# Large products as Strassen blocks of seven half products, in four passes over the tokens, with transposes finished by DMA

## The chip, the core and the metric

The kernel runs on one core of one Trainium2 chip. A core has TensorE (PE, matmuls into PSUM; PEld is its weight load), VectorE (DVE), ScalarE (ACT), GpSimd (POOL) and SyncE (SP, which here issues all DMAs), and 16 DMA engines that move data between HBM and SBUF. The engines run side by side, each through its own list of instructions in a fixed order, and wait for one another by semaphores. The metric is the device time of one execution in microseconds, as the median of several runs.

## The reference, cut to what matters

One layer of a decoder trunk over 4096 tokens of 1024 features. A projection gives u, v (768 columns each), queries q_x (256) and a gate (1024). A gated spatial mixing and a 4-head cross-attention into a memory of 256 tokens stand side by side, both are multiplied by the SiLU of the gate and sent through an output projection, residual and layer norm.

```python
proj = jnp.einsum('bsd,de->bse', x, a_w_in[j])
u, v, q_x, gate = split_cols(proj, [TOK_WIDTH, TOK_WIDTH, XATTN_WIDTH, MIX_WIDTH])
tok = chunked_spatial_gating(u, v, a_w_s[j], a_b_s[j])
...
xo = memory_cross_attention(q_x, mem_k, mem_v)
mixed = jnp.concatenate([tok.astype(x.dtype), xo.astype(x.dtype)], axis=-1) * jax.nn.silu(gate)
y = jnp.einsum('bse,ed->bsd', mixed, w_out[i]).astype(x.dtype)
x = layer_norm(ALPHA * x + y, ln_g[i], ln_b[i])
```

The spatial gating takes GELU of u and v, normalises v in groups of 128 features, multiplies it with a causal 128 x 128 matrix within each chunk of 128 tokens, and multiplies the result with u.

## The kernel before

[...] To keep precision, every operand is split into a high part (a cast on ScalarE, L48) and a low part (a subtraction on VectorE, L49), and each product is made of three matmuls: high x high, high x low, low x high (`mm3`, L93 to L101). The contraction over 1024 features is 8 steps of 128.

Work goes over 16 blocks of 256 tokens, in three phases:

1. Phase 1 (p1) computes v and u by tokens (`by_token`: 2 halves of 128 tokens, 2 x 384 columns, tile `pair`), then GELU, the group norm (`v_norm`), the mixing (`mix`, L194) and the product with u. The result is transposed to features on partitions by VectorE in 32 x 32 blocks, 16 instructions for each half of a block (`block_transpose`, L119, tile `zt`), and stored to HBM (`z1_d`).
2. Phase 2 (p2) computes the gate by features (`by_feature`, 256 tokens as columns, tile `single`), and the attention: queries (`q_part`), scores (`scores`, L315), softmax, the transpose of the probabilities (L119, tile `pt`), their split into `pT` (L48, L49) and the product with the values (`attend`, L337). Attention of one block is spread between the gate products of the same and the next block.
3. Phase 3 (p3) does the output projection by tokens (512 columns), residual and layer norm.

Weights stay in SBUF (`wt`), and their columns are replaced by the next phase's while the former phase still runs. x is loaded from HBM in phases 1 and 2 and split again each time. A scheduler that simulates the program sets the order of the instructions on each engine; on the chip each engine follows that order and only waits. SP is one such list: a DMA that waits for its data holds back all DMAs behind it.

## Time and profile before

| | us |
|---|---|
| median of 3 runs | 1515.41 |
| lowest and highest run | 1514.56, 1518.41 |
| span of the profiled execution (first to last instruction) | 1513.3 |
| TensorE busy | 1462.3 (97%) |
| VectorE busy | 1082.4 (72%) |
| ScalarE busy | 446.8 (30%) |
| GpSimd busy | 207.2 (14%) |
| DMA, mean rate | 98 GB/s |

Busy time counts an engine's own instructions; matmuls are pipelined, so a busy TensorE is not one at its peak. The granted clock is given as a share of 2.4 GHz. A stretch of the profile is named by microseconds from the span's start. Phase 1 ends near 600 us and phase 2 near 1145 us in this execution.

### The profile page before, as it was taken

What the parts mean: (1) busy time and instruction counts of PE and PEld (TensorE: products, weight loads), DVE (VectorE), ACT (ScalarE), POOL (GpSimd) and SP (SyncE); (2) the same over time, 40 slices, a digit from 0 to 9 for tenths busy, and PEclk for the clock granted to TensorE, in tenths of its full rate; (3) what the DMA queues carried; (4) which work ended last, traced back from release to release, by engine and by line L of the source; (5) the groups of instructions that cost most, each with busy time, mean ns of one, the idle gap of its engine ahead of it and who ended that gap; (6) DMA issues with size and microseconds to landing.
All of it is one profiled execution on the core that took longest, in us unless ns stands there. A gap on an engine that the chain in (4) does not pass through costs nothing.

```text
span 1513.3 us, 24060 instructions
## 1 busy us (share of the span) xinstructions
PE 1462.3 (97%) x9392; PEld 1386.7 (92%) x9392; DVE 1082.4 (72%) x2606; ACT 446.8 (30%) x850; POOL 207.2 (14%) x149
## 2 busy tenths in 40 slices
PE   8999999999999999989999999999998999999997
PEld 8999999999999999889999999999997888888886
DVE  7767777777767777877888877777775656566564
ACT  5222222211232223454544444554441011011010
POOL 1000000000000000222222222222220100000000
PEclk9999999999999999999999999999999999999999
DMA  7222222211222224332233323222234544444331
GB/s 253 63 57 57 65 68 57 64 52 49 63 68 70 66 64 129 93 95 93 75 100 110 95 94 99 86 92 83 86 105 154 174 139 135 143 144 141 133 132 56
DMA packets 96466, 147.71 MB, mean 98 GB/s; under 512 B 8160, under 2 KB 40416, under 8 KB 96352
## 3 DMA queue, kind: packets, MB, share of 16 engines
q1 hardware_dynamic: 96352, 146.18, 30.7%
q8 instruction: 73, 1.20, 0.3%
q14 instruction: 41, 0.34, 0.1%
HBM read 100.01 MB, written 46.14 MB: 97 GB/s over the span
## 4 chain that ended last, share of the span: by engine, by line
PE 64%; DVE 24%; ACT 5%; issue 3%; DMA 2%; POOL 2%; SPq 0%; DVEq 0%; POOLq 0%; ACTq 0%
PE pair L99 55%; DVE pt L119 14%; PE single L99 5%; DVE zt L119 2%; POOL p L326 2%; PE single L194 2%; PE pair L315 2%; ACT p L323 2%; DVE xt L49 1%; DVE pT L49 1%; ACT xt L48 1%; DVE zx L344 1%; ACT L323 1%; DMA raw<-xT 1%; DVE wt L49 1%
## 5 line engine op out<-in xcount | busy, mean ns | idle before, releaser
L99 PE MATMUL pair<-wt,xt 128*128 128x384 f32 (+1 forms) x4560 | 886.4, 356 | 6.4 <-ACT wt L48 6.4
L99 PEld LDWEIGHTS pair<-wt,xt 128*128 128x128 f32 x4560 | 813.9, 189 | 74.4 <-ACT wt L48 6.4
L99 PE MATMUL single<-xt,wt 128*128 128x256 f32 x3888 | 473.6, 281 | 2.0 <-DVE xt L49 1.8
L99 PEld LDWEIGHTS single<-xt,wt 128*128 128x128 f32 x3888 | 463.9, 189 | 4.4 <-DVE xt L49 4.0
L119 DVE STREAM_TRANSPOSE pt<-p 32x256 f32<-32x256 f32 x512 | 223.2, 436 | 12.8 <-POOL p L326 5.7
L48 ACT CAST xt<-raw 128x512 fp32r<-128x512 f32 x196 | 112.7, 621 | 362.3 <-PE pair L99 204.0
L119 DVE STREAM_TRANSPOSE zt<-u 32x192 f32<-32x192 f32 x512 | 189.2, 370 | 6.9
L49 DVE TENSOR_TENSOR xt<-raw,xt 128x512 fp32r<-128x512 f32 x196 | 131.2, 691 | 32.2 <-ACT xt L48 31.3
L412 DVE SCALAR_TENSOR_TENSOR rr<-xr,pair 128x512 f32<-128x512 f32 x62 | 39.9, 683 | 130.2 <-PE pair L99 119.4
L182 POOL TENSOR_TENSOR rs<-rs,mhalf 128x6 f32<-128x6 f32 x32 | 43.8, 1370 | 530.9 <-DVE rs L181 500.2
L307 POOL TENSOR_TENSOR z<-z,g 128x512 f32<-128x512 f32 x48 | 73.3, 1527 | 273.4 <-ACT g L300 237.2
L199 DVE SCALAR_TENSOR_TENSOR u<-single,bs,u 128x256 f32<-128x256 f32 x96 | 40.5, 478 | 79.2 <-ACT u L258 77.6
L48 ACT CAST pT<-pt 128x1024 fp32r<-128x1024 f32 x32 | 33.5, 1047 | 160.5 <-DVE pt L119 160.5
L326 POOL TENSOR_TENSOR p<-p,sm 128x1024 f32<-128x1024 f32 x32 | 60.0, 1894 | 150.5 <-DVE sm L325 131.6
L417 POOL TENSOR_TENSOR rs<-rs,mhalf 128x1 f32<-128x1 f32 x32 | 29.0, 905 | 341.2 <-DVE rs L416 308.5
L184 DVE TENSOR_SCALAR vg<-vg,mv,rs 128x128 f32<-128x128 f32 x192 | 52.2, 342 | 32.2 <-POOL rs L182 32.0
L315 PE MATMUL pair<-kst,qs 128*128 128x256 f32 x256 | 43.2, 291 | 26.7 <-DVE qs L163 25.8
L173 ACT ACTIVATE vg<-pair 128x768 f32<-128x768 f32 x32 | 26.0, 814 | 134.4 <-DVE st L177 89.4
L315 PEld LDWEIGHTS pair<-kst,qs 128*128 128x128 f32 x256 | 35.3, 192 | 30.3 <-DVE qs L163 29.2
L323 ACT ACTIVATE p<-pair,nm 128x256 f32<-128x256 f32 x128 | 58.6, 484 | 0.2
L48 ACT CAST vn<-vg 128x768 fp32r<-128x768 f32 x32 | 26.7, 836 | 98.8 <-DVE vg L184 74.8
L258 ACT ACTIVATE u<-pair 128x768 f32<-128x768 f32 x32 | 25.9, 810 | 91.9 <-PE pair L99 91.9
(56 smaller groups left out, 814.2 us busy)
## 6 DMA issues: line engine op xcount, KB each, us to landing
raw<-xT SPq DMA_DIRECT2D x128, 256.0 KB, 3.4
raw<-zd SPq DMA_DIRECT2D x64, 256.0 KB, 3.5
xr<-x SPq DMA_DIRECT2D x32, 512.0 KB, 3.5
out<-rr SPq DMA_DIRECT2D x62, 256.0 KB, 2.6
z1d<-zt SPq DMA_DIRECT2D x32, 384.0 KB, 2.9
z<-z1d SPq DMA_DIRECT2D x48, 256.0 KB, 2.9
zd<-z SPq DMA_DIRECT2D x48, 256.0 KB, 2.4
raw<-w_in SPq DMA_DIRECT2D x20, 256.0 KB, 3.3
```

Source lines behind the costliest of these rows:

```text
L48: nc.scalar.copy(hi, src)
L49: eng.tensor_tensor(lo, src, r(hi), op=ALU.subtract)
L99: nc.tensor.matmul(o, stat(sh, k), mv(mh, k), start=(k == 0 and sh == 0 and mh == 0), stop=(k == KD - 1 and sh == 1))
L119: nc.vector.transpose(dst[j:j + 32, :, i:i + 32], src[i:i + 32, :, j:j + 32])
L182: nc.gpsimd.tensor_tensor(rs, rs, mhalf, op=ALU.pow)
L184: nc.vector.tensor_scalar(vg[:, g, :], vg[:, g, :], mv[:, g, 0:1], rs[:, g:g + 1], op0=ALU.subtract, op1=ALU.mult)
L199: nc.vector.scalar_tensor_tensor(u[:, :, gs], ps[:, j], bs[:, g:g + 1], u[:, :, gs], op0=ALU.add, op1=ALU.mult)
L307: nc.gpsimd.tensor_tensor(z, z, g, op=ALU.mult)
L315: nc.tensor.matmul(pv[:, h, :], qs[:, h, c * P:(c + 1) * P], kst[:, i, h, :], start=(i == 0), stop=(i == 1))
L323: nc.scalar.activation(p[:, h, :], pv[:, h, :], AF.Exp, bias=nm[:, h:h + 1], scale=SCALE, accum_out=sm[:, h:h + 1])
L326: nc.gpsimd.tensor_tensor(p, p, sm.unsqueeze(2).broadcast_to([P, HEADS, M]), op=ALU.mult)
L412: nc.vector.scalar_tensor_tensor(rr[:, cs], xr[:, cs], ALPHA, y, op0=ALU.mult, op1=ALU.add)
```

## The change

The four large products (u, v, queries and gate from x; output from the mixed features) are computed by a Strassen scheme (the Winograd form with 7 products and 15 additions). For a block of 256 tokens the left operand is cut into 2 x 2 quarters (128 tokens x 512 features), the weights into quarters of 512 features x n columns. Seven parts of each are formed (`x_parts`, `w_parts`: 4 additions each on GpSimd), split into high and low, and 7 products over 512 features (`product`, 12 matmuls each) go to three PSUM accumulators, whose sums are finished on ScalarE, VectorE and GpSimd (`gemm`).

All seven weight parts of a product fill SBUF (`arena`, 8 slots of 16 KB a partition), so the work is cut into four passes over all tokens, `places` saying where each pass's weights lie:

1. g = 0: the first 384 columns of v and of u, and the queries. It also forms the weight parts of passes 2 and 3 on the side (`prepare_slice`) and stores them in HBM (`w_d`).
2. g = 1: the other 384 columns of v and u, and the gate of the attention. It stores the seven parts of x in HBM (`x_d`, 3.67 MB a block) and prepares the weight parts of pass 4.
3. the gate of the 768 mixed features (384 columns a half) and the attention. The parts of x come back from HBM (`load_x`), unsplit work is not repeated.
4. the output projection, residual and norm.

Transposes are made in two steps: VectorE transposes 32 x 32 blocks in place of all 128 partitions in one instruction (`transposed`), and DMA moves the blocks to their places in HBM (`scatter`, four DMAs with pieces of 256 bytes; the queries of pass 1 with pieces of 128 bytes in eight), from where they are loaded again: the queries (`q_d`), the probabilities (`p_d`), the attention gate (`gx_d`) and the gated features (`z_d`).

```diff
-    def mm3(outs, stat, movs, ks=range(KD)):
...
+    def product(acc, t, w, first):
+        for k in range(KH):
+            for i, (a, b) in enumerate(((0, 0), (0, 1), (1, 0))):
+                nc.tensor.matmul(acc, t[:, a, k, :], w[:, b, k, :], start=first and k == 0 and i == 0,
+                                 stop=k == KH - 1 and i == 2, skip_group_check=True)
...
+        ax = acc("accx")
+        product(ax, xs[0], ws[0], True)
+        s1 = cs()
+        nc.scalar.copy(s1, ax)
+        aw = acc("accw")
+        product(aw, xs[1], ws[1], True)
+        u2 = cs()
+        nc.vector.tensor_tensor(u2, aw, s1, op=ALU.add)
...
+        product(aw, xs[4], ws[4], False)
+        nc.vector.tensor_tensor(s5, aw, s5, op=ALU.add)
+        done(1, 1, s5)
...
+    def x_parts(r0, r1):
+        a11, a21 = r0[:, :, :P], r0[:, :, P:]
+        a12, a22 = r1[:, :, :P], r1[:, :, P:]
+        s1, s2, s3, s4 = (sum_tile() for _ in range(4))
+        tt = nc.gpsimd.tensor_tensor
+        yield a11
+        tt(s1, a21, a22, op=ALU.add)
+        tt(s2, s1, a11, op=ALU.subtract)
+        yield s2
...
+    def parts_of(src, make):
...
+        for part in make(*load_pair(src[:, :KH, :], src[:, KH:, :])):
+            t = ring()
+            split(t[:, 0], t[:, 1], part)
+            tiles.append(t)
...
+    def first_weights():
+        for j in range(WIDTH[0] // P):
+            js = slice(j * P, (j + 1) * P)
+            for i, part in enumerate(w_parts(*load_pair(wl[SLICE0[0] + j, 0], wl[SLICE0[0] + j, 1]))):
+                w = view(places[0][i], WIDTH[0])
+                split(w[:, 0, :, js], w[:, 1, :, js], part)
...
+    def prepare_slice(n):
...
+            t = ring()
+            split(t[:, 0], t[:, 1], part)
+            nc.sync.dma_start(w_d[g][i][:, :, :, js], f(t))
...
+    def scatter(dst, src):
...
+        dv = dst.rearrange("k (j i) (q s) -> q i (k j) s", j=4, q=4)
+        for q in range(4):
+            nc.sync.dma_start(dv[q], src[q * 32:(q + 1) * 32].rearrange("i j c t -> i j (c t)"))
...
-    def block_transpose(dst, src):
-        """dst[c, g, t] = src[t, g, c] for every g, as 32 x 32 blocks."""
-        for i in range(0, P, 32):
-            for j in range(0, P, 32):
-                nc.vector.transpose(dst[j:j + 32, :, i:i + 32], src[i:i + 32, :, j:j + 32])
...
+                    nc.vector.tensor_reduce(nm, ps, axis=AX.X, op=ALU.max)
+                    nc.vector.tensor_scalar(nm, nm, -SCALE, None, op0=ALU.mult)
+                    p = sum_tile().rearrange("p k c -> p (k c)").rearrange("p (h m) -> p h m", h=2)
...
+                    nc.gpsimd.tensor_tensor(p, p, sm.unsqueeze(2).broadcast_to([P, 2, M]), op=ALU.mult)
+                    transposed(pts[hp], p.rearrange("p h m -> p (h m)"), c)
+            for hp in range(2):
+                scatter(p_d[b % 2][4 * hp:4 * hp + 4], pts[hp])
+
+        def weights_of(b):
+            nc.sync.dma_start(f(pT[:, 1]), p_d[b % 2].rearrange("k p t -> p k t"))
+            split(pT[:, 0], pT[:, 1], f(pT[:, 1]))
...
+            gemm(psum, xs, ws, 384, done)
+            scatter(z_d[b][:NH], zt)
+            attend(b, gx)
+            if b + 1 < NB:
+                scores(b + 1)
+                weights_of(b + 1)
```

The pool `ringp` holds 9 part tiles (two more than a block's seven), `raw` 3 tiles, `sums` 3 tiles; `pT` and the query tiles lie in `arena`, one and two of them.

How the order of the built program differs is shown at two places. On TensorE, in the stretch of gate and attention: scores (`sc`, before `pair<-kst,qs`) and attention products (`at`, before `pair<-pT,vst`) stand among the gate products. Before, one block's round, which repeats to the end of the stretch:

```order
L99 MATMUL single<-xt,wt 128x256 x66
L337 MATMUL pair<-pT,vst 128x256 x16
L99 MATMUL single<-xt,wt 128x256 x141
L315 MATMUL pair<-kst,qs 128x256 x4
L99 MATMUL single<-xt,wt 128x256 x12
```

After, the last gate products (`accw`, `accq`, 384 columns) and what follows them:

```order
L162 MATMUL accq<-arena,xc 128x384 x12
L408 MATMUL at<-arena 128x256 x2
L381 MATMUL sc<-arena 128x256 x4
L408 MATMUL at<-arena 128x256 x14
L162 MATMUL accw<-arena,xc 128x384 x12
L381 MATMUL sc<-arena 128x256 x12
```

The 12 `accw` matmuls there are the last gate product of the sixteenth block, and the 16 `at` around them are the fifth attention round. From there on 12 `sc`, 2 `at`, 4 `sc` and 14 `at` come in turn until the sixteenth round, with no other matmul between them; the first of the output projection stands behind the last. So what was spread among gate products now stands, for 11 of 16 blocks, alone.

On SP, in the same stretch. Before, the DMAs of one block's gate products and attention (loads of x and z1, stores of z):

```order
L308 DMA zd_94<-z 128x512 [waits Pool_49]
L305 DMA z<-z1d_79 128x512 [waits DMAHW4_49,DMAHW3_49]
L78 DMA raw<-xT 128x512 [waits DMAHW5_49,DVE_49]
L69 DMA raw<-w_out 128x512 [waits DMAHW6_49,DVE_49]
L69 DMA raw<-w_out 128x256 [waits DMAHW7_49,DVE_49]
L308 DMA zd_95<-z 128x512 [waits Pool_49]
```

After, one of the rounds behind the gate products (`pd` are the scattered probabilities in HBM, `arena<-pd` the load of pT, `arena<-qd` that of the next queries):

```order
L373 DMA arena<-qd_118 128x4x256 [waits PE_49]
L416 DMA zd_147<-zx 128x2x256 [waits DVE_49]
L430 DMA gx<-gxd_133 128x2x256 [waits Activation_49]
L213 DMA pd_266<-raw 32x16x64 [waits DVE_49]
L213 DMA pd_266<-raw 32x16x64 x3
L213 DMA pd_266<-raw 32x16x64 [waits DMAHW2_49,DVE_49]
L213 DMA pd_266<-raw 32x16x64 [waits DMAHW3_49]
L213 DMA pd_266<-raw 32x16x64 [waits DMAHW4_49]
L213 DMA pd_266<-raw 32x16x64 [waits DMAHW5_49]
L398 DMA arena<-pd_266 128x8x256 [waits DMAHW4_49,DMAHW5_49,DMAHW3_49,DMAHW6_49,DMAHW2_49,DMAHW7_49,DMAHW1_49,DMAHW0_49]
```

The probabilities went from VectorE to ScalarE within SBUF before. Now they leave by eight stores, and their load stands behind all eight landings.

On VectorE, in the same stretch. Before, around the transposes of one block's probabilities (`pt<-p`), with the low parts of x (`xt<-raw`) between:

```order
L319 TENSOR_REDUCE nm<-pair 128x4 x2
L320 TENSOR_SCALAR nm<-nm 128x4 x2
L49 TENSOR_TENSOR xt<-raw,xt 128x512 x3
L325 RECIPROCAL sm<-sm 128x4 x2
L119 STREAM_TRANSPOSE pt<-p 32x8x32 x16
```

After, from one block's low part of pT (`arena<-arena`) through the first transpose for the next block's scatter (`raw<-sums`):

```order
L69 TENSOR_TENSOR arena<-arena 128x2048
L385 TENSOR_REDUCE nm<-sc 128x2
L386 TENSOR_SCALAR nm<-nm 128x2
L391 RECIPROCAL sm<-sm 128x2
L414 TENSOR_TENSOR zx<-at,zx 64x256
L200 STREAM_TRANSPOSE raw<-sums 128x16x32
L414 TENSOR_TENSOR zx<-at,zx 64x256 x2
L385 TENSOR_REDUCE nm<-sc 128x2 x2
```

Three more transposes follow, and then the next low part of pT: four quarters of the next scores (two heads and 128 tokens each) now stand between one low part and the next.

## Rows read from the trace of the kernel before

**Rows 1.** The page: busy time, share of the span, instructions; granted clock by slice.
```profile
PE 1462.3 (97%) x9392; PEld 1386.7 (92%) x9392; DVE 1082.4 (72%) x2606; ACT 446.8 (30%) x850; POOL 207.2 (14%) x149
...
PEclk9999999999999999999999999999999999999999
```

**Rows 2.** Busy time of each engine in three stretches; then clock, DMA share, GB/s.
```profile
200.00:400.00 200.00, 200.00 (x1195) 200.00 (x1194) 141.24 (x464) 42.04 (x60) 15.86 (x12) 1.00 0.20 54
800.00:1000.00 200.00, 191.92 (x1613) 189.49 (x1612) 155.36 (x311) 96.30 (x212) 52.09 (x30) 1.00 0.30 96
1200.00:1400.00 200.00, 200.00 (x859) 161.04 (x858) 119.54 (x215) 20.62 (x36) 16.44 (x18) 1.00 0.42 142
```

**Rows 3.** The chain that ended last, phase 1: start, us, engine, tile, line.
```profile
327.09 33.30 PE pair L99 x192
360.39 2.14 PE single L194 x18
```

**Rows 4.** Groups by form: count, busy us, mean ns, idle before (matmul, transposes, splits, GpSimd).
```profile
L99 PE MATMUL single<-xt,wt 128*128 128x256 f32 x3888 | 473.6, 281 | 2.0 <-DVE xt L49 1.8 <-DVE u L199 0.2
L119 DVE STREAM_TRANSPOSE pt<-p 32x256 f32<-32x256 f32 x512 | 223.2, 436 | 12.8 <-POOL p L326 5.7
L119 DVE STREAM_TRANSPOSE zt<-u 32x192 f32<-32x192 f32 x512 | 189.2, 370 | 6.9
L49 DVE TENSOR_TENSOR xt<-raw,xt 128x512 fp32r<-128x512 f32 x196 | 131.2, 691 | 32.2 <-ACT xt L48 31.3
L307 POOL TENSOR_TENSOR z<-z,g 128x512 f32<-128x512 f32 x48 | 73.3, 1527 | 273.4 <-ACT g L300 237.2 <-DMA z<-z1d 36.2
```

**Rows 5.** Groups by form, attention: exponentials, GpSimd product, reduction, splits, 64-partition operand.
```profile
L326 POOL TENSOR_TENSOR p<-p,sm 128x1024 f32<-128x1024 f32 x32 | 60.0, 1894 | 150.5 <-DVE sm L325 131.6 <-DMA raw<-xT 18.9
L323 ACT ACTIVATE p<-pair,nm 128x256 f32<-128x256 f32 x128 | 58.6, 484 | 0.2
L49 DVE TENSOR_TENSOR pT<-pt,pT 128x1024 fp32r<-128x1024 f32 x32 | 40.4, 1263 | 2.0 <-ACT pT L48 1.5
L319 DVE TENSOR_REDUCE nm<-pair 128x4 f32<-128x1024 f32 x32 | 37.7, 1220 | 15.3 <-PE pair L315 15.1
L48 ACT CAST pT<-pt 128x1024 fp32r<-128x1024 f32 x32 | 33.5, 1047 | 160.5 <-DVE pt L119 160.5
L163 DVE TENSOR_TENSOR qs<-single,qs 64x256 fp32r<-64x256 f32 x64 | 27.0, 422 | 12.5 <-ACT qs L162 11.3
```

**Rows 6.** Timeline at 883 us: start, duration, engine, line, operation.
```profile
883.61 0.18 DVE L325 RECIPROCAL sm<-sm 128x4 f32<-128x4 f32 x1 [2.39 <-ACT p L323]
...
883.87 3.75 POOL L326 TENSOR_TENSOR p<-p,sm 128x1024 f32<-128x1024 f32 x2 [9.73 <-DVE sm L325]
```

**Rows 7.** DMA from 336 to 342 us: packets, share of 16 engines, issue, us to landing.
```profile
DMA packets 784, 0.39 MB, mean 66 GB/s; under 512 B 16, under 2 KB 784, under 8 KB 784
...
q1 hardware_dynamic: 784, 0.39, 22.4%
...
z1d<-zt SPq DMA_DIRECT2D x1, 384.0 KB, 2.8
```

**Rows 8.** DMA from 0 to 12 us: packets, MB, share of 16 engines.
```profile
DMA packets 1445, 3.53 MB, mean 294 GB/s; under 512 B 127, under 2 KB 127, under 8 KB 1445
...
q1 hardware_dynamic: 1445, 3.53, 81.4%
```

**Rows 9.** The page's DMA issues: count, KB each, median us to landing.
```profile
xr<-x SPq DMA_DIRECT2D x32, 512.0 KB, 3.5
```

**Rows 10.** Timeline at the start: the first matmuls.
```profile
6.37 7.95 PE L99 MATMUL pair<-wt,xt 128*128 128x384 f32 x36 [6.37 <-ACT wt L48]
```

**Rows 11.** Stretches after the last matmul, columns as in rows 2.
```profile
1505.00:1508.00 3.00, 0.00 (x0) 0.00 (x0) 2.90 (x9) 0.00 (x0) 0.65 (x1) 0.99 0.00 0
1508.00:1511.00 3.00, 0.00 (x0) 0.00 (x0) 1.33 (x4) 0.00 (x0) 0.00 (x0) 0.50 0.51 175
```

More of the change, by code (lines that the diff above doesn't have):

```diff
@@ L17 @@
 KD = D // P
+KH = KD // 2
 TOK = 768
@@ L25 @@
 NB = T // TB
-CW = 384
-WC = 2048
-KVB = 10
 EPS = 1e-5
@@ new lines, in prepare_slice, with weights @@
+    def prepare_slice(n):
+        g = max(i for i in range(4) if SLICE0[i] <= n)
+        j = n - SLICE0[g]
+        js = slice(j * P, (j + 1) * P)
+        for i, part in enumerate(w_parts(*load_pair(wl[n, 0], wl[n, 1]))):
+            t = ring()
+            split(t[:, 0], t[:, 1], part)
+            nc.sync.dma_start(w_d[g][i][:, :, :, js], f(t))
+    def weights(g, load=True):
+        ws = [view(o, WIDTH[g]) for o in places[g]]
+        if load:
+            for w, d in zip(ws, w_d[g]):
+                nc.sync.dma_start(f(w), d)
+        return ws
@@ new lines, in transposed @@
+    def transposed(dst, src, c):
+        nc.vector.transpose(dst[:, :, c, :], src)
+    z1_d = [dram.tile([P, 2, TOK], F32, name=f"z1d{b}") for b in range(NB)]
+    q_d = [dram.tile([HEADS, P, TB], F32, name=f"qd{b}") for b in range(NB)]
+    gx_d = [dram.tile([2, P, TB], F32, name=f"gxd{b}") for b in range(NB)]
+    z_d = [dram.tile([KD, P, TB], F32, name=f"zd{b}") for b in range(NB)]
+    x_d = [[dram.tile([P, 2, KH, P], F32, name=f"xd{b}_{i}") for i in range(7)] for b in range(NB)]
+    p_d = [dram.tile([2 * HEADS, P, TB], F32, name=f"pd{i}") for i in range(2)]
@@ L384, in trunk_kernel @@
+    with tc.tile_pool(name="fin", bufs=1) as pool, \
+            tc.tile_pool(name="acc3", bufs=8, space=bass.MemoryType.PSUM) as psum:
+        ws = weights(3)
+        nxt = parts_of(z_d[0].rearrange("k p t -> p k t"), x_parts)
+        lg = pool.tile([P, D], F32, name="lg")
+        lb = pool.tile([P, D], F32, name="lb")
         nc.sync.dma_start(lg, ln_g.partition_broadcast(P))
         nc.sync.dma_start(lb, ln_b.partition_broadcast(P))
+        H = D // 2
         for b in range(NB):
-            nxt = load_xt(z_d[b + 1]) if b + 1 < NB else None
@@ new lines, in trunk_kernel @@
+            add = nc.gpsimd.tensor_tensor
+            ax = acc("accx")
+            product(ax, xs[0], ws[0], True)
+            s1 = cs()
+            nc.scalar.copy(s1, ax)
+            b12, b22 = cs(), cs()
+            add(b12, s1, xr[0][:, H:], op=ALU.add)
+            aw = acc("accw")
+            product(aw, xs[1], ws[1], True)
+            nc.vector.tensor_tensor(b12, aw, b12, op=ALU.add)
+            aq = acc("accq")
+            product(aq, xs[2], ws[2], True)
+            nc.scalar.copy(b22, aq)
@@ new lines, in trunk_kernel @@
+            add(b22, b22, s1, op=ALU.add)
+            add(b22, b22, xr[1][:, H:], op=ALU.add)
+            add(s1, s1, xr[1][:, :H], op=ALU.add)
+            product(ax, xs[3], ws[3], False)
+            done(0, 0, ax, xr[0][:, :H])
+            product(aw, xs[4], ws[4], False)
+            done(1, 1, aw, b22)
+            product(aq, xs[5], ws[5], False)
+            done(0, 1, aq, b12)
+            finish(0)
+            product(aw, xs[6], ws[6], False)
+            done(1, 0, aw, s1)
+            finish(1)
@@ L434 @@
     x = np.ascontiguousarray(inputs["x"]).reshape(T, D)
+    w_in = np.asarray(inputs["a_w_in"])[0]
+    w_out = np.asarray(inputs["w_out"])[0]
+    u, v, q, g = np.split(w_in, [TOK, 2 * TOK, 2 * TOK + XW], axis=1)
+    gx = g[:, TOK:]
+    halves = [
+        (np.concatenate([v[:, :384], q[:, :P]], 1), np.concatenate([u[:, :384], q[:, P:]], 1)),
+        (np.concatenate([v[:, 384:], gx[:, :P]], 1), np.concatenate([u[:, 384:], gx[:, P:]], 1)),
+        (g[:, :384], g[:, 384:TOK]),
+        (w_out[:, :512], w_out[:, 512:]),
+    ]
+    slices = []
+    for n0, n1 in halves:
+        for j in range(n0.shape[1] // P):
+            s = np.concatenate([n0[:, j * P:(j + 1) * P], n1[:, j * P:(j + 1) * P]], 1)
+            slices.append(s.reshape(2, KH, P, 2 * P).transpose(0, 2, 1, 3))
     arrays = {
```

627 lines of the change are left out of this document (305 added, 322 removed).

## The prediction

> **What bounds the kernel now.** I read the page's busy shares first, then the chain of work that ended last, then the busy time by stretch, then single prices. TensorE is busy 1462.3 us of a span of 1513.3 us and its granted clock never leaves the top tenth [rows 1]. In the first and last third of the work it has no gap at all: 200.00 us of 200. Only the attention stretch loses 4%, and there VectorE is at 78% [rows 2]. The chain runs block after block on TensorE: 192 products of 384 columns take 33.30 us, 18 of 256 columns 2.14 us [rows 3]. So today the time is the count of matmuls times their price, plus about 50 us. DMA moves little: 0.20 to 0.42 of its engines' time [rows 2].
>
> Prices of one matmul follow: 384 columns 33.30 / 192 = 0.173 us, 256 columns 2.14 / 18 = 0.119 us [rows 3], 512 columns 200 / 859 = 0.233 us [rows 2].
>
> **What the change takes off TensorE.** Seven half products replace eight. A block of 256 tokens needs 7 x 4 x 3 = 84 matmuls per pass: 16 x 84 x 3 = 4032 of 512 columns, 1344 of 384, and 896 of 256 (mixing 288, scores 256, attention 256, memory 96). That is 4032 x 0.233 + 1344 x 0.173 + 896 x 0.119 = 1279 us against 1462: 183 us less. Also gone are 1024 transposes of 32 partitions (223.2 + 189.2 us [rows 4]); transposes of 128 partitions, 0.3 us for 128 columns and 0.7 for 512 by the step between those two rows (1 ns a column), take their place, and DMA finishes them. What the change adds I price stage by stage, because the matmul time is no longer the end of every stage.
>
> **What a DMA packet costs.** One store of 512-byte pieces kept the 16 engines busy 22.4% of 6 us for 784 packets: 16 x 6 x 0.224 / 784 = 27.4 ns each, at 502 bytes on average. The first 12 us give 16 x 12 x 0.814 / 1445 = 108 ns at 2443 bytes [rows 7, 8]. The line through both is 6.5 ns + 0.0416 ns a byte: 177 ns for 4 KB, 49 for 1 KB, 17 for 256 bytes, 12 for 128. The kernel before moves nothing in pieces of 128 or 256 bytes, so these lie between the line's 6.5 ns at no bytes and, if small packets are dearer, twice the 512-byte price, 55 ns. I take the line, since the nearest row is on it, and keep both ends.
>
> **Lead-in, 31 us** (today TensorE starts at 6.37 us [rows 10]). The first product needs part 1 of all four weight slices, the second the GpSimd sums of the last slice. A slice is four chained GpSimd additions of 512 columns; the nearest row is 1.53 us [rows 4], and three raw buffers for two loads a slice leave one load of 3.5 us [rows 9] half uncovered each time. Four slices end near 28 us, the second product begins near 33, the first took 2.8 of that. Bounds 28 to 36.
>
> **Pass 1 of 4, 344 us.** A block is 84 x 0.233 + 9 x 0.119 = 20.6 us of TensorE, 330 us in all. VectorE has some 15.3 us a block (7 low parts at 0.691 us [rows 4], 4 additions from PSUM at the same price, 1.4 of transposes, some 6 of norm and mixing) and 20.2 in the 7 blocks that prepare a slice. That is 85%, so I charge the 4% that the attention stretch loses at 78% [rows 2]: 330 / 0.96 = 344. DMA needs 45 us of engine time a block for x, 18 for z1, 4096 x 12 = 49 for the queries and 245 for each of 7 prepared slices (7168 pieces of 512 bytes): 3507 / 16 = 219 us, hidden. If VectorE held nothing up it is 330; if the full blocks cost 5 us each, 365.
>
> **Pass 2, 350 us.** Same TensorE time. DMA now also stores all seven parts of x: per block 896 packets of 4 KB, 256 for the next x, 256 of 1.5 KB, 1024 of 256 bytes: 240 us of engine time, 16 blocks 3832; four prepared slices add 978 and the loads of the next weights (14.7 MB) 611. Sum 5421 / 16 = 339 us of DMA beside 344 on TensorE. Two resources that both need the whole stage do not overlap perfectly; 350, bounds 339 and 370.
>
> **Pass 3 up to its last gate product, 337 us.** The order of the built program puts all x loads behind the last store of pass 2: last norm, store and first loads are about 22 us (2.8 us for a store to land [rows 7], 3.5 for a load [rows 9], 3 MB queued ahead of the first product, and some 8 us of norm). Then, per block: x back 159 us of engine time, z1 34, scattered zt 3072 x 17 = 53: 246 / 16 = 15.4 us, 246 us for 16 blocks. Five attention rounds stand between these blocks, each with 25 for queries, 50 for pT, 70 for the scattered probabilities (4096 x 17) and 25 for gate and result: 170 / 16 = 10.7 us, 53 in all. Weights ahead: 16. Together 22 + 315 = 337. TensorE needs only 22 + 16 x 84 x 0.173 + 5 x 3.8 = 274, so DMA is the bound here. Bounds 290 and 385.
>
> **The attention tail, 302 us. This term decides.** The order on TensorE has 5 of the 16 attention rounds between the gate products and 11 after the last of them, with nothing else on TensorE until the output projection. And a round can't overlap the next: SP loads the transposed weights only when all eight scattered stores have landed, into the only pT; on VectorE the low part of pT stands ahead of the next scores' reductions and transposes, and those ahead of the next scatter. So a round is one loop of waits, priced from [rows 5] unless noted, halves taken where the operand is half:
> - high part of 2048 columns on ScalarE, from 1.047 us for 1024: 1.9; low part on VectorE, from 1.263: 2.4.
> - first quarter of the next scores: six matmuls at the lower clock 1.4 (TensorE idles most of a round; at the end of the kernel, idle too, its granted clock reads 0.99 and then 0.50, that is 1.2 GHz [rows 11]), reduction 0.65, scaling 0.2, two exponentials 1.1, reciprocal 0.2, GpSimd product 0.95, transpose 0.7: 5.2.
> - the other three quarters, interleaved with the additions of the last attention: VectorE alone needs 3 x 0.42 + 3 x 0.65 + 0.6 + 0.7 + 0.5 + 3 x 0.7 = 7.1, with waits 7.7.
> - last four stores 1.3 to issue and 2.8 to land [rows 7], 4.1; load of 1 MB: a fixed 2.1 (3.5 us less the packets of 512 KB [rows 9]) and 1024 packets at 49 ns, 3.1, together 5.2.
> - ten hand-offs at 0.1, as from VectorE to GpSimd in [rows 6]: 1.0.
> Sum 27.5 us, of which TensorE works 4. Eleven rounds: 302 us. In the kernel before the same chain ran behind gate products and cost the stretch only the 4%. Bounds per round: 24 (no hand-offs, loads at their best) and 32 (dearer small packets), so 264 to 352.
>
> **Last pass, 326 us, and end, 8 us.** TensorE 16 x 84 x 0.233 = 313 us; VectorE has about 17 us a block of 19.6 (7 low parts, 5 additions, 4 statistics, four passes over 1024 columns at 1.3, by [rows 4, 5]), so again 4%: 326. The end is the last norm and its store: two passes at 1.3, 2 us of statistics and additions, 1 on GpSimd, 2.8 to land.
>
> **Sum.** 31 + 344 + 350 + 337 + 302 + 326 + 8 = 1698 us of span. The median of the runs shown is 2 us over the profiled span (1515.41 and 1513.3), so 1700 us, 12% slower. All low bounds together give 28 + 330 + 339 + 290 + 264 + 313 + 8 = 1572, all high ones 36 + 365 + 370 + 385 + 352 + 345 + 10 = 1863; they won't all fall to one side.
>
> **Rivals.**
> Faster: the rounds pipeline after all. p_d and the query buffers are doubled, and with two rounds in flight one costs half, 13.7 us: the tail is 151. If pass 3 is then bound by TensorE (274) and passes 1, 2 and 4 lose nothing (330, 339, 313), the sum is 31 + 330 + 339 + 274 + 151 + 313 + 8 = 1446. Against it: pT is single, and VectorE's order is fixed. With my other terms, a round has to fall under (302 - 185) / 11 = 10.7 us for the change to win, which two DMA landings alone (2.8 + 5.2) nearly fill.
> Dear small packets, at 55 ns: zt costs 7.3 us more a block (+116), five rounds between the blocks 9.7 each (+49), each tail round 7.3 (+80), pass 2's gate scatter +39, and pass 1's scattered queries, 128 bytes, make its DMA 398 us (+54): 1700 + 338 = 2040 us. For it: 12 of a block's 24 DMAs in pass 3 are such stores. Against it: down to 512 bytes the price falls in step with the size, with no sign of a floor.
> The Trainium skill, "DMA: Bandwidth & Descriptors", section Specifications, names 512 bytes as the least transfer for line rate and says that below it the engine reads, modifies and writes. That rule speaks against this change's scatter, no data row of this trace reaches below 512 bytes to test it, and by it the sum would be this rival's.
> No saving on TensorE: if 12 products in a row into one bank ran slower than today's alternation of two, the three wide passes would grow. The 256-column groups already run 24 in a row into one bank at 473.6 / 3888 = 0.122 us [rows 4], so I give it nothing of its own.
>
> **How the numbers follow.** Serial tail, 1590 to 1810: 0.82. Dear packets, up to 2040: 0.10. Pipelined rounds: 0.08, three quarters of it faster. Range 1590 to 1810, which leaves 0.2 outside. About 0.3% can be told from no change: faster 0.06, within 0.01, slower 0.93.
>
> **What the profile after would show.** TensorE near 1280 us busy and about 75% of the span; a stretch near 300 us, before the output projection, where TensorE is at a tenth or two, the clock at its lower level and DMA under half; a pass before it with DMA over 0.9; the 256-byte stores at near 17 ns. I am wrong if attention rounds in that stretch come every 15 us or less, or if the scatter, not the loop, takes most of a round, or if passes 1 and 2 lose much more than 4% to VectorE.

## The result: 19% slower, at the upper edge of the range

The changed kernel takes 1808.9 us (median of 3 runs, 1808.45 to 1810.32), 1.193 times the kernel before (95% interval 1.191 to 1.195). 1700 us was forecast, with a range of 1590 to 1810. The direction and the deciding mechanism came as forecast; the time lies only 1 us inside the range. The profiled execution has a span of 1806.4 us, where the sum gave 1698.

The page of the changed kernel, the parts that answer [rows 1] (busy shares; then the span in 40 slices of 45.2 us):

```profile
PE 1384.3 (77%) x6272; PEld 1148.8 (64%) x6272; DVE 1135.8 (63%) x2092; ACT 739.5 (41%) x1505; POOL 753.4 (42%) x562
...
PE   1999999989899999789998981132323399898886
...
PEclk9999999999999999889999985555555699999998
DMA  4477776799999899999999997434343755454443
```

TensorE, which was at nine tenths or more almost throughout, starts a slice later, sags at the start of pass 3 (slices 17 and 18), and has a hole of eight slices at one to three tenths, where its clock is granted at 0.5 (1.2 GHz) for most of the way. The same by stretch, inside each pass (busy time of each engine, granted clock, DMA share, GB/s), as [rows 2] did for the kernel before:

```profile
60.00:400.00 340.00, 319.79 (x1384) 246.92 (x1383) 261.59 (x565) 184.83 (x410) 166.63 (x117) 1.00 0.74 199
404.00:752.00 348.00, 334.83 (x1487) 270.43 (x1488) 241.76 (x552) 171.75 (x345) 158.54 (x109) 0.99 0.97 335
...
752.00:790.00 38.00, 21.26 (x111) 19.42 (x109) 13.34 (x34) 12.92 (x27) 1.33 (x1) 0.73 0.97 377
...
790.00:1080.00 290.00, 265.71 (x1505) 260.03 (x1506) 119.81 (x241) 112.22 (x232) 95.96 (x96) 0.96 1.01 336
1080.00:1430.00 350.00, 86.53 (x351) 73.31 (x349) 136.99 (x259) 121.54 (x274) 60.62 (x55) 0.54 0.48 136
1454.00:1776.00 322.00, 288.22 (x1175) 225.46 (x1174) 280.34 (x340) 97.19 (x155) 207.99 (x140) 0.97 0.47 133
```

Rows one to six are pass 1, pass 2, the gap behind it, pass 3 up to its last gate product, the attention tail and pass 4. In the tail no engine is busy for even 40% of the time and DMA for half: everything waits. The boundaries are read from the matmuls of the four large products: passes 1 and 2 end with their last product, passes 3 and 4 begin with their first.

| stage | forecast us | measured us | difference |
|---|---|---|---|
| lead-in and pass 1 | 31 + 344 = 375 | 402.9 | +28 |
| pass 2 | 350 | 349 | -1 |
| pass 3 to its last gate product (gap, then gate) | 22 + 315 = 337 | 38.7 + 289.7 = 328.4 | -9 |
| attention tail, to the first product of pass 4 | 302 | 351 | +49 |
| pass 4 | 326 | 364.4 | +38 |
| end | 8 | 10.5 | +2 |

One round of the tail, in order of time (start, duration, engine, line, output and input; in brackets the idle time before and what ended it):

```profile
1254.81 0.38 SPq L398 DMA_DIRECT2D arena<-pd  x1
1260.56 1.90 ACT L68 CAST arena<-arena 128x2048 fp32r<-128x2048 f32 x1 [10.22 <-DMA arena<-pd]
1262.49 2.29 DVE L69 TENSOR_TENSOR arena<-arena 128x2048 fp32r<-128x2048 f32 x1 [13.79 <-ACT arena L68]
...
1265.69 1.28 ACT L389 ACT_TABLE_LOAD   x1 [3.23 <-DVE nm L386]
...
1277.68 5.08 SPq L213 DMA_DIRECT2D pd<-raw  x8
1278.26 0.71 DVE L200 STREAM_TRANSPOSE raw<-sums 128x512 f32<-128x512 f32 x1 [0.61 <-POOL sums L392]
...
1284.82 0.38 SPq L398 DMA_DIRECT2D arena<-pd  x1
```

From the issue of one load of pT to the next are 30.0 us. The load takes 5.75 us to the cast behind it; from the last transpose's end (1278.97) to the next load, which waits for all eight scattered stores, are 5.85 us: 11.6 us of a round are DMA. Nine of the eleven rounds take 29 to 30 us, the first and the last 40.

TensorE's waits in 1080 to 1430 us (what it waited for, us in total, times, longest) say the same:

```profile
PE at L408 <- ACT arena L68: 227.6, 11, 32.2
```

### The profile page after: what moved, and what is told of

The parts are those of the page before. It is cut to its first block, busy times and chain, and to the rows that moved or that the text cites. A ratio compares the mean times of both kernels' runs of the same rounds, so it can differ in the third digit from the quotient of the medians.

```text
span 1806.4 us, 20514 instructions
## 1 busy us (share of the span) xinstructions
PE 1384.3 (77%) x6272; PEld 1148.8 (64%) x6272; DVE 1135.8 (63%) x2092; ACT 739.5 (41%) x1505; POOL 753.4 (42%) x562
## 4 chain that ended last, share of the span: by engine, by line
PE 27%; DMA 19%; DVE 18%; ACT 8%; issue 8%; SPq 7%; POOL 5%; POOLq 0%; DVEq 0%; ACTq 0%
PE accw L162 12%; PE accq L162 7%; PE accx L162 7%; SPq L213 5%; DMA arena<-pd 5%; DVE xc L69 3%; DMA raw<-xT 3%; DVE xr L496 2%; DMA xr<-x 2%; DMA xc<-xd 2%; ACT vg L294 2%; DVE nm L385 2%; DMA pd<-raw 2%; DVE arena L69 2%; ACT sums L389 1%
## 5 line engine op out<-in xcount | busy, mean ns | idle before, releaser
L162 PE MATMUL accw<-arena,xc 128*128 128x512 f32 (+1 forms) x2304 | 554.0, 388 | 51.8 <-DVE cs L510 19.6
L162 PEld LDWEIGHTS accw<-arena,xc 128*128 128x128 f32 x2304 | 426.7, 192 | 143.2 <-DVE cs L510 23.6
L162 PE MATMUL accx<-arena,xc 128*128 128x512 f32 (+1 forms) x1536 | 380.7, 389 | 61.0 <-ACT xc L68 35.7
L162 PE MATMUL accq<-arena,xc 128*128 128x512 f32 (+1 forms) x1536 | 365.5, 384 | 11.0 <-ACT cs L184 7.5
L162 PEld LDWEIGHTS accx<-arena,xc 128*128 128x128 f32 x1536 | 287.1, 192 | 119.3 <-ACT xc L68 37.4
L162 PEld LDWEIGHTS accq<-arena,xc 128*128 128x128 f32 x1536 | 285.8, 191 | 64.3 <-ACT cs L184 9.8
L69 DVE TENSOR_TENSOR xc<-sums,xc 128x512 fp32r<-128x512 f32 x236 | 199.0, 855 | 119.4 <-ACT xc L68 111.5
L68 ACT CAST xc<-sums 128x512 fp32r<-128x512 f32 x236 | 141.3, 616 | 184.9 <-POOL sums L79 62.3
L69 DVE TENSOR_TENSOR xc<-raw,xc 128x512 fp32r<-128x512 f32 x189 | 162.8, 866 | 72.1 <-ACT xc L68 72.0
L68 ACT CAST xc<-raw 128x512 fp32r<-128x512 f32 x189 | 115.3, 617 | 82.1 <-PE accw L162 16.0
```

Of the source, the lines that this page charges most:

```text
L68: nc.scalar.copy(hi, src)
L69: nc.vector.tensor_tensor(lo, src, f(hi), op=ALU.subtract)
L162: nc.tensor.matmul(acc, t[:, a, k, :], w[:, b, k, :], start=first and k == 0 and i == 0, stop=k == KH - 1 and i == 2, skip_group_check=True)
```

## Experiments on the attention tail

Each experiment up to the joined versions is a single run; eleven runs of the kernel before lie within 3.7 us of one another.

**Theory:** the round is a loop of waits, closed by the way of the probabilities through DRAM. **Rivals:** DMA or an engine is simply busy that long; or the way through DRAM is one long link among others.

### The load reads the other buffer

```
-            nc.sync.dma_start(f(pT[:, 1]), p_d[b % 2].rearrange("k p t -> p k t"))
+            nc.sync.dma_start(f(pT[:, 1]), p_d[(b + 1) % 2 if b else 0].rearrange("k p t -> p k t"))
```

> Each attention round loads its transposed probabilities from the other of the two scratch buffers in DRAM, which holds the round before it (so the result is that of shifted weights). Traffic, pieces, instructions and engines are the same; only the wait of the load for this round's eight scattered stores is gone. In the built order 8 attention rounds (not 11) stand behind the last gate product. Theory (a loop of waits: scatter 5.85 us and load 5.75 us of the 29.5 us round): a round behind the gate products falls to 18 to 24 us, since the load may start as soon as the product before has read the one tile, and the whole span falls by 80 to 170 us, to 1640 to 1730. Rival (the DMA engines or the other engines are simply busy that long): a round stays at 28 to 30 us and the sum of gate part and tail stays within 20 us of 636.

Measured: span 1647.7 us, 159 less. The attention products of seven rounds in the tail, changed kernel first, then this one (duration of one; first and last start):

```profile
L408 PE MATMUL at<-arena x112: 415/415/583, 1115.4 to 1297.8; 128*128 128x256 f32 x112
```
```profile
L408 PE MATMUL at<-arena x112: 280/415/584, 1148.9 to 1249.9; 128*128 128x256 f32 x112
```

Six periods and one round's own products (some 5 us) lie in 182 and in 101 us: 29.5 against 16.0 us a round. The edit takes away nothing but a wait, and 13.5 us of a round went, more than the theory's 5.5 to 11.5, because scores, transposes and stores now run beside load and split. The order of the built program followed the edit: 8 rounds instead of 11 stand behind the gate products, and in some rounds VectorE's low part stands ahead of the last transpose of the round. So the 13.5 us are the wait together with the order that it had forced. The traffic and the instructions are those of the changed kernel; DMA bandwidth and engine work are excluded as the cause. Gate part and tail together fell from 641 to 465 us, and pass 4 gave 16 us of this back.

### No way through DRAM: TensorE transposes

```
-                    transposed(pts[hp], p.rearrange("p h m -> p (h m)"), c)
-            for hp in range(2):
-                scatter(p_d[b % 2][4 * hp:4 * hp + 4], pts[hp])
...
+                    tp = oth("tp")
...
+                            nc.tensor.transpose(tp[:, e, ms], p[:, e, ms], ident)
...
+                    split(hi, lo, tp.rearrange("p e (m q t) -> p (e m) q t", m=2, q=4))
```

> The probabilities no longer pass through DRAM: TensorE transposes them (16 transposes of 128x128 a round, through PSUM), ScalarE and VectorE split them from PSUM into the one tile. The 32 scattered stores' pieces and the 1 MB load of a round are gone (95 of 170 us of DMA engine time), TensorE gets some 3.4 us a round more. 9 rounds stand behind the last gate product in the built order. Theory: a round behind the gate products is then bound by its engines, VectorE some 9 us, ScalarE some 9, TensorE at its lower clock some 10, so 10 to 15 us; tail 9 x 12 = 110 instead of 346, gate part 280 to 300; span 1540 to 1620. Rival (the round is long for the engines' sake, softmax and the table load, not for the way through DRAM): rounds of 18 us or more, span over 1640.

Measured: span 1697.6 us; 9 rounds behind the gate products, still 29 us each. The forecast round of 10 to 15 us was wrong. The rival's numbers came (18 us or more, over 1640), but its reason, the engines' work, did not: in 220 us of this tail no engine is busy for 40% (TensorE 80.9, VectorE 71.1, ScalarE 83.3 us) and DMA is nearly idle:

```profile
1090.00:1310.00 220.00, 80.87 (x354) 72.36 (x352) 71.13 (x169) 83.27 (x206) 34.10 (x33) 0.56 0.15 46
```
```profile
PE tp L400 <- POOL sums L395: 135.3, 30, 6.7
```

The second row is TensorE's wait. The timeline shows why it is so long:

```profile
1219.36 1.11 PE L400 MATMUL tp<-ident,sums 128*128 128x128 f32 x4 [5.88 <-POOL sums L395]
...
1220.12 1.20 PE L384 MATMUL sc<-arena 128*128 128x256 f32 x4
...
1225.26 1.12 PE L400 MATMUL tp<-ident,sums 128*128 128x128 f32 x4 [3.94 <-POOL sums L395]
```

In TensorE's fixed order the transposes of one quarter stand ahead of the scores of the next. So scores, reduction, exponentials, GpSimd product and transposes of the four quarters form one chain of 5.9 us each. One loop of waits had gone, another of the same length had come.

### The order turned

The code emits the scores of the next quarter ahead of this quarter's transposes, and one PSUM bank more goes to the attention.

```
+            prev = None
+            for c in range(2):
+                for hp in range(2):
+                    p = first(c, hp)
+                    if prev:
+                        second(*prev)
+                    prev = c, hp, p
+            second(*prev)
```

> As e2_pe_transpose, but the code puts the scores of the next quarter ahead of the transposes of this one, and the attention has four PSUM banks instead of three (the gate products four instead of five). Traffic, instruction counts and results are those of e2_pe_transpose. In the built order 4 rounds (not 9) stand behind the last gate product. Theory, revised after e2: the round there was 29 us because the fixed order on TensorE made its four quarters one chain of some 5.9 us each (scores, reduction, exponentials, GpSimd product, transposes), so it is a chain of waits again and no engine's work. With two quarters under way a round takes 15 to 20 us, gate part and tail together 380 to 420 instead of 530 (e2) and 641 (the changed kernel), the span 1530 to 1600. Rival (an engine's work bounds the round, the table loads and softmax on ScalarE): rounds stay above 25 us and the span above 1640.

Measured: span 1552.0 us. From the first gate product to the first product of pass 4 are 394 us, where the changed kernel has 641. Four rounds are left behind the gate products, 17 to 24 us each. Beside the gate products TensorE is now the bound, at 307 of 318 us and full clock, with DMA at 0.92 close behind:

```profile
790.00:1108.00 318.00, 307.05 (x1925) 302.33 (x1924) 166.38 (x388) 225.77 (x471) 128.14 (x126) 0.99 0.92 308
1108.00:1183.00 75.00, 38.85 (x184) 33.35 (x182) 41.44 (x92) 44.10 (x108) 23.93 (x22) 0.64 0.49 166
```

With the same instructions as the run with TensorE's transposes (1697.6 us), the order (and the bank) alone gave 146 us. The two were not tried apart.

### Gate products held back until the attention has run

```
-            zt = pool.tile([P, 24, 2, 32], F32, name="zt")
+            zt = pool.tile([P, 24, 2, 32], F32, name="zt", tag="zz")
-            zx = pool.tile([P, 2, TB], F32, name="zx")
+            zx = pool.tile([P, 2, TB], F32, name="zx", tag="zz")
```

> Only one thing is changed: the gate's transposed tile and the attention's result tile share one buffer, so a gate block's end waits for the attention of the block before, and 12 of 16 attention rounds (not 5) stand between the gate products. Nothing is taken away. Theory (the round is a loop of waits that costs TensorE nothing while gate products stand beside it): pass 3 becomes 16 rounds of 28 to 32 us, 450 to 520 with the gap ahead of it apart, instead of 290 + 346 = 636; span 1640 to 1690. Rival (both parts are bound by DMA, which is full beside the gate products): the rounds between the gate products stretch to 36 us and more, and the span stays over 1760.

Measured: span 1835.1 us, 29 more than the changed kernel; rounds between gate products took 40 us. My theory fell. The rival's numbers came (over 36 us, over 1760), but DMA was not full, at 0.73 of the stretch 916 to 1324 us. What TensorE waited for there, and what that waited for in turn:

```profile
PE accq L162 <- ACT cs L184: 191.6, 11, 22.4
ACT cs L184 <- POOL z L440: 128.5, 11, 17.3
POOL z L440 <- DMA z<-z1d: 102.0, 10, 15.5
```

SP's list in one round shows where that load stands:

```profile
1063.78 6.79 SPq L213 DMA_DIRECT2D pd<-raw  x8
...
1072.02 1.09 SPq L428 DMA_DIRECT2D z<-z1d  x1
```

The load of z1 reuses a buffer that the tied transposes free late, and stands on SP behind the scattered stores, eight of which take 6.8 us to issue. So with the tie the attention's stores stand on the gate's path. How much of the wait is the buffer and how much the queue, this run does not tell apart.

The same tie on the kernel without the stores of probabilities:

> As e5_order, with the one shared buffer of e3_tie (the gate's transposed tile and the attention's result): 2 rounds instead of 4 behind the last gate product. Without the way through DRAM, SP has no scattered stores of probabilities ahead of the load of z1, which the products of e3_tie waited for. Theory: the tie now costs nothing much and takes off part of the tail: 0 to 25 us less than e5_order. Rival (any tie between gate and attention makes TensorE wait, whatever the queue): 15 us or more slower than e5_order.

Measured: span 1569.9 us against 1552.0 without the tie, 18 us slower, so the theory is wrong and the rival's number came, though narrowly: from the first gate product to the first of pass 4 the tie cost 12.5 us, and the other 5.4 lie in passes that it does not touch. With the way through DRAM gone, GpSimd waited 17.6 us in the gate part for the load of z1 instead of 102.0, so that way had made most of the wait. TensorE's largest wait there was now for GpSimd's product in the softmax, 13.2 us against 3.3 without the tie.

## Experiments on the pace of passes 1 and 4

In the changed kernel, VectorE's instructions with both operands in SBUF take longer than [rows 4, 5] show, and those that read PSUM do not. Pass 4 (mean ns behind the comma):

```profile
L496 DVE SCALAR_TENSOR_TENSOR xr<-xr,rs,lb 128x1024 f32<-128x1024 f32 x28 | 59.0, 2107 | 6.1 <-POOL rs L494 6.1
L69 DVE TENSOR_TENSOR xc<-sums,xc 128x512 fp32r<-128x512 f32 x56 | 53.4, 953 | 5.8 <-ACT xc L68 5.5
L495 DVE SCALAR_TENSOR_TENSOR xr<-xr,mv,lg 128x1024 f32<-128x1024 f32 x28 | 44.8, 1600 | 0.0
...
L487 DVE TENSOR_TENSOR xr<-accw,cs 128x512 f32<-128x512 f32 x29 | 19.7, 679 | 4.0 <-POOL cs L515 4.0
```

**Theory:** GpSimd, busy 42% of the span instead of 14%, holds VectorE up wherever both of VectorE's operands lie in SBUF. **Rivals:** the strided source, ScalarE, DMA, or a slow supply of x.

### The dispute measured by itself

> A kernel of its own that computes nothing of the reference: rows of single instructions, one kind after another, with a join of the engines between the kinds. VectorE's low part of 512 columns with both operands in SBUF: alone, from a strided operand, with one operand in PSUM; a 1024-column scalar_tensor_tensor alone; then each of these beside GpSimd additions of 512 columns, and the first beside ScalarE copies and beside loads by DMA. Theory (GpSimd slows VectorE where both of VectorE's operands lie in SBUF): 0.69 us alone and 0.8 us or more beside GpSimd; scalar_tensor_tensor 1.3 us alone and 1.6 or more beside GpSimd; with one operand in PSUM 0.67 both times; no change beside ScalarE or DMA. Rival 1 (the strided source): 0.85 us strided and alone. Rival 2 (ScalarE or DMA traffic): 0.8 us or more beside one of these.

Measured (lines 72, 75, 78, 81: alone; strided and alone; one operand in PSUM and alone; 1024 columns and alone. Lines 87, 92, 97: beside GpSimd, 92 with one operand in PSUM. Line 101: beside ScalarE; 108: beside DMA loads):

```profile
L87 DVE TENSOR_TENSOR lo<-a,hi 128x512 fp32r<-128x512 f32 x24 | 27.9, 1162 | 0.8
L97 DVE SCALAR_TENSOR_TENSOR lo<-a,hi 128x1024 fp32r<-128x1024 f32 x12 | 25.1, 2088 | 0.4
L101 DVE TENSOR_TENSOR lo<-a,hi 128x512 fp32r<-128x512 f32 x24 | 16.6, 693 | 0.8
L108 DVE TENSOR_TENSOR lo<-a,hi 128x512 fp32r<-128x512 f32 x24 | 16.6, 692 | 0.8
L92 DVE TENSOR_TENSOR lo<-ps,hi 128x512 fp32r<-128x512 f32 x24 | 16.6, 691 | 0.8
L72 DVE TENSOR_TENSOR lo<-a,hi 128x512 fp32r<-128x512 f32 x20 | 13.8, 692 | 0.7
L75 DVE TENSOR_TENSOR lo<-sa,hi 128x512 fp32r<-128x512 f32 x20 | 13.8, 692 | 0.6
L78 DVE TENSOR_TENSOR lo<-ps,hi 128x512 fp32r<-128x512 f32 x20 | 13.8, 691 | 0.6
L81 DVE SCALAR_TENSOR_TENSOR lo<-a,hi 128x1024 fp32r<-128x1024 f32 x10 | 12.3, 1226 | 0.3
```

The theory holds, and the strided source, ScalarE and DMA fall as rivals: 512 columns take 691 to 693 ns in every case but the one beside GpSimd with both operands in SBUF. (A slow supply of x can't show in this kernel; the run without GpSimd's sums bears on it.) The mean of 1162 ns mixes two stretches, while GpSimd had additions left and after its last one:

```profile
L87 DVE TENSOR_TENSOR lo<-a,hi x12: 1632/1632/1634, 79.0 to 97.4; 128x512 fp32r<-128x512 f32 x12
L87 DVE TENSOR_TENSOR lo<-a,hi x11: 691/692/693, 99.0 to 106.3; 128x512 fp32r<-128x512 f32 x11
```

From the second instruction on, which is the first to start with GpSimd's additions under way, each of twelve took 1632 to 1634 ns (the numbers are the smallest, median and largest duration, then the first and last start). They start every 1.67 us, in turn with GpSimd's additions, which take 1.59 us here and 1.26 alone: the two engines take turns, instruction by instruction. Of the twelve instructions of 1024 columns (line 97), all but the first took 2.17 us.

The Trainium skill, "SBUF — State Buffer", section "Who interferes with whom", says that a VectorE instruction with two SBUF inputs contends with a GpSimd instruction that reads SBUF, and that one with at most one SBUF input, outside VectorE's two-port modes, does not. Its section "Summary: rules for kernel authors" says that the second of the two to issue is blocked until the first has finished. The run agrees with the first two (1632 ns against 691, and 691 from PSUM). With the third it agrees nearly: a pair takes 1.67 us, under the 0.69 + 1.26 = 1.95 of both alone, so the two overlap a little.

### Gain and bias of the last norm in PSUM

```
+        nc.scalar.copy(lgp, lg)
+        nc.scalar.copy(lbp, lb)
-                nc.vector.scalar_tensor_tensor(r, r, mv[:, i, 0:1], lg, op0=ALU.subtract, op1=ALU.mult)
-                nc.vector.scalar_tensor_tensor(r, r, rs[:, i:i + 1], lb, op0=ALU.mult, op1=ALU.add)
+                nc.vector.scalar_tensor_tensor(r, r, mv[:, i, 0:1], lgp, op0=ALU.subtract, op1=ALU.mult)
+                nc.vector.scalar_tensor_tensor(r, r, rs[:, i:i + 1], lbp, op0=ALU.mult, op1=ALU.add)
```

> The changed kernel with one thing else in its last pass: gain and bias of the last norm are copied to PSUM once, so that the two passes of 1024 columns have one operand in SBUF and one in PSUM (four banks go to this; the products keep four instead of eight). Theory (GpSimd and VectorE exclude each other where both of VectorE's operands lie in SBUF; the last pass has 9.7 us of such VectorE work and some 12 us of GpSimd work in a block of 19.6): the two passes fall from 1.60 and 2.11 us to 1.2 to 1.3, the low parts beside them from 0.95 to 1.1 toward 0.75 to 0.9, the pass from 364 us to 322 to 345, the span to 1765 to 1790. Rival (the block waits for something else, DMA or the number of GpSimd steps in a row): the pass stays over 355 us.

Measured: pass 4 takes 332 us instead of 364, the span is 1773.3. The two passes over 1024 columns take 1.27 us each, near the 1.23 measured alone; the second:

```profile
L500 DVE SCALAR_TENSOR_TENSOR xr<-xr,rs,lbp 128x1024 f32<-128x1024 f32 x29 | 37.0, 1275 | 2.3 <-POOL rs L498 1.3
```

The low parts beside them stayed slow (0.96 and 0.90 us), more than expected. The edit also leaves the products four PSUM banks instead of eight, which was not tried apart.

### The x parts without GpSimd's sums

```
-        tt(s1, a21, a22, op=ALU.add)
-        tt(s2, s1, a11, op=ALU.subtract)
-        yield s2
-        yield s1
+        yield a21
+        yield a22
```

(and likewise for s3 and s4)

> The changed kernel without the four GpSimd sums of the x parts (and of the z parts in the last pass): the parts are taken from the loaded tile as they are, so the products are not Strassen's and the result is another; count and shape of all other work are the same. Theory (GpSimd's sums slow VectorE's low parts and final passes): low parts go back to 0.69 to 0.75 us where no weights are prepared, pass 1 ends at 375 to 390 instead of 403, the last pass takes 318 to 335 instead of 364, the span is 1735 to 1765. Rival (the passes lose their pace to the supply of x, loads and buffers): pass 1 and the last pass stay within 8 us of what they are.

Measured: pass 1 ends at 388.7 us instead of 402.9, as the theory has it, with the loads of x unchanged; but the last pass takes 360 us instead of 364, as the rival has it, and the span is 1782.5. In the last pass the contention had only moved: the second norm pass took 2.23 us there, even longer than before, beside GpSimd's additions of the residual. It and TensorE's wait behind it:

```profile
L490 DVE SCALAR_TENSOR_TENSOR xr<-xr,rs,lb 128x1024 f32<-128x1024 f32 x27 | 60.3, 2234 | 4.9 <-POOL rs L488 4.9
```
```profile
PE accw L156 <- DVE cs L504: 28.2, 11, 3.7
```

TensorE waited for an addition on VectorE that comes after the norm of the block before. So in the last pass it is the norm, not the sums, that has to be kept out of GpSimd's way.

## What came of joining them

> e5_order and e6_norm_psum joined, and two further GpSimd additions given to VectorE with one operand in PSUM (the third product's copy plus sum in the gemm of passes 1 to 3, the same in the last pass). Theory: the gains are on different stretches and add up: pass 3 as in e5_order (394 to 402 us from first gate product to last product of the pass before the last), last pass 325 to 335 us, pass 1 ends at 390 to 400; span 1508 to 1532, time within 1% of the kernel before. Rival (VectorE, which takes the additions, becomes the bound of passes 1 and 4): last pass over 345, pass 1 no earlier than 403, span over 1545.

Measured: 1512.0 us (median of 8 runs), 0.9968 of the kernel before (0.9957 to 0.9979). Pass 1 ends at 396, pass 3 takes 393 from its first gate product, pass 4 takes 325: the gains add up as expected.

The second one also moves DMA work from a full pass to one with room:

```
-                if g == 1:
+                if g == (0 if b < 6 else 1):
                     for i, t in enumerate(xs):
                         nc.sync.dma_start(x_d[b][i], f(t))
```

> As e8_joined, with the x parts of the first six blocks stored in pass 1 instead of pass 2 (22 MB, some 59 us of all 16 DMA engines moved from a pass with a share of 0.97 to one with 0.74). 3 rounds instead of 4 stand behind the last gate product in the built order. Theory (pass 2 is bound by DMA, and its 13 us stall behind the third block is SP waiting for room in its queue): pass 2 falls from 347 to 333 to 340 us, pass 1 gains nothing and loses under 5; the time is 8 to 20 us under e8_joined, 1490 to 1515. Rival (the stores hold the ring's buffers, so pass 1 loses as much as pass 2 gains): within 5 us of e8_joined.

Measured: 1498.05 us (median of 4 runs), 0.9878 of the kernel before (0.9863 to 0.9893): a version that beats both. Against the first joined version, pass 2 takes 334 us from its first product to its last instead of 347, and the gap behind it 32 instead of 39; pass 1 pays 2. Pass 4 takes 332 instead of 325, which is not explained. Passes 1 and 2 in this version, to be held against the first two rows of the table by stretch above:

```profile
60.00:398.00 338.00, 317.75 (x1393) 251.81 (x1392) 274.42 (x583) 178.02 (x393) 147.15 (x105) 0.99 0.86 252
402.00:735.00 333.00, 331.40 (x1483) 268.88 (x1482) 251.62 (x571) 166.39 (x332) 129.26 (x90) 1.00 0.85 286
```

TensorE has no gap left in pass 2. So the scheme gains on this chip once its side work is out of the way, and then 1.2%.

## Why the prediction was right, and where its sizes were wrong

**That the range held was in part luck.** The time lies 1 us under its upper end: lead-in and pass 1, the tail and pass 4 took 115 us more than their terms, pass 2 and pass 3 up to its last gate product 10 us less. One of the prediction's own signs of being wrong came true: pass 1 lost 10%, where the sum allowed 4% for VectorE. TensorE was busy 1384 us, not near 1280. In the tail, at a granted clock of 0.54, its 351 matmuls of 256 columns took 86.5 us, 0.25 each instead of 0.119, and the rest is spread over the other stretches.

**The mechanism held.** The tail of eleven serial rounds is the largest loss, and it is a loop of waits: the first experiment took away one wait, and the order that came with it, with all work left, and the tail's round fell from 29.5 to 16 us. The saving on TensorE is real as well. One product's twelve matmuls into one bank start 2.80 us apart, 0.233 us each, so the rival of no saving is out:

```profile
1512.34 2.96 PE L162 MATMUL accw<-arena,xc 128*128 128x512 f32 x12
1515.14 2.96 PE L162 MATMUL accq<-arena,xc 128*128 128x512 f32 x12
```

**The tail, 302 forecast, 351 measured.** The order of the built program was read rightly (11 rounds). A round was 2 us too short: ScalarE's load of its table for the exponential (1.28 us) stands on the path, since it starts only when the exponential is ready, and issue and landing of the stores took 5.85 us, not 4.1, the load 5.75, not 5.2; other terms came out shorter. Two rounds of 40 us, the first and the last, and 5 us before pass 4 were not foreseen; why they were so long stays open.

**Passes 1 and 4, 66 us more than forecast with the lead-in: the step that failed.** The sum took VectorE's prices from a kernel whose GpSimd is busy 14% of the span, and charged 4% for a VectorE at 85%. With GpSimd three times as busy, those prices no longer held: in pass 4 a low part took 0.95 us instead of 0.69, and the norm's passes 1.60 and 2.11 instead of 1.3. Pass 1 loses 10% (22.8 us a block from the second on, against 20.6), pass 4 18% (23.05 against 19.56). Keeping the norm out of GpSimd's way gave back 32 us of pass 4's 38, and taking GpSimd's sums of x away gave 14 us in pass 1; what is left of pass 1's loss was not followed. The lead-in, by its rows, is the same step, though no run tried it: the second product began at 43.3 us instead of 33. It was priced by GpSimd's chain at 31 us, while VectorE was busy for 25.9 of the 26 us ahead of the first product, at nearly twice its price in [rows 4]:

```profile
L69 DVE TENSOR_TENSOR arena<-sums,arena 128x512 fp32r<-128x512 f32 x12 | 14.3, 1223 | 0.1
```

**Pass 2, 350 forecast, 349 measured, by the reason given:** DMA at 0.97. Moving stores out of it made it TensorE's again.

**Pass 3 to its last gate product, 337 against 328.4: right by two errors.** The gap was priced at 22 us for norm, landing and 3 MB ahead of the first product. It took 38.7 with DMA at 0.97 and 377 GB/s: 14 MB went by (38 us at that rate), stores of pass 2, the next weights and the memory's inputs among it. In the chain of waits the load of the queries stands there for 22.5 us.

The gate part took 289.7 us instead of 315, with DMA at 1.01, that is full: DMA was the bound as forecast. Less of the summed work fell into it: nine of the 112 loads of x parts had been issued in the gap, and nine of the 64 stores of gated features came after its end, by the sum's own prices some 20 of the 25 us.

**Small packets cost nearly what the line said.** In 8 us that hold one scatter's stores (4096 pieces of 256 bytes, and the end of other transfers):

```profile
DMA packets 4977, 1.78 MB, mean 222 GB/s; under 512 B 4272, under 2 KB 4976, under 8 KB 4976
...
q1 hardware_dynamic: 4976, 1.77, 92.5%
```

16 x 8 x 0.925 / 4976 = 23.8 ns a packet at 356 bytes; the line gives 21.3, the rival of dear packets 55. The Trainium skill, "DMA: Bandwidth & Descriptors", section Specifications, from which the prediction took that rival, names 512 bytes as the least transfer for line rate and says that below it the engine reads, modifies and writes. A lower rate shows here (222 GB/s against 377 in the gap ahead of pass 3), about as the line has it; a jump in price below 512 bytes does not.

**Pipelined rounds** did not come. Of the reasons named, the load's wait for all eight landings is the one that was tried: without it rounds came every 16 us, with pT still single.

## What to carry to other kernels

When a change takes work off the engine that bounds the kernel, write out what each block then asks of the engines beside it, with the prices they will have in the new mix: GpSimd work is not free where VectorE reads two operands from SBUF, and keeping one of them in PSUM gave back 32 us here. A chain of small dependent steps that other work used to hide costs its full length once the order puts it behind that work, and taking one long wait out of it may only bring the next to light: look at the fixed order on the engine that idles before changing what it does. Holding the other work back to cover such a chain made it worse here, by 29 us with the way through DRAM and by 12 in that stretch without it, because one shared buffer made each of the two wait for the other.

## What the runs showed of the hardware

- VectorE and GpSimd take turns, instruction by instruction, where both of VectorE's operands lie in SBUF and GpSimd adds from SBUF: 512 columns of VectorE take 1632 ns instead of 691, GpSimd's 1588 instead of 1262. VectorE work of 1.23 us (1024 columns) takes 2.17.
- Neither a strided source, nor ScalarE, nor DMA loads into SBUF changed VectorE's 692 ns.
- A short gap of TensorE can cost more than its length. In pass 4, after a gap of 3.3 us, the granted clock was 0.50 (1.2 GHz) from 1498.7 to 1502.0 us, and 20 matmuls of 512 columns took 7.7 us, where 24 take 5.76 at the full clock. After a gap of 2.6 us in pass 2 the clock stayed at 1.00, and twelve took 3.07 us, near the 2.96 without a gap. The two rows of pass 4:

```profile
1498.73 7.70 PE L162 MATMUL accw<-arena,xc 128*128 128x512 f32 x20 [3.30 <-DVE xr L487]
...
1520.27 5.76 PE L162 MATMUL accw<-arena,xc 128*128 128x512 f32 x24
```

- SP's issue of a DMA is not free: eight stores of 128 KB in pieces of 256 bytes took 5.1 us of SP in the tail, and 6.8 beside other traffic, where the load of 1 MB took 0.38. Why these took longer stays open.
